# Down projection of a hybrid block: the products M3 and M7 change places in the order of the seven

## The chip, the cores and the metric

The program runs on one core of a Trainium2 chip. The metric is the time of one execution on the device in microseconds. The engines are PE (TensorE; PEld is its weight load), DVE (VectorE), ACT (ScalarE), POOL (GpSimd) and SP (SyncE, which here only issues transfers). Each works through its own list of instructions in order, and semaphores tie the lists together.

## The reference

One block of a hybrid model on 512 tokens of width 2048 in float32: a norm, an input projection, a state-space mixer and a sparse attention side by side, an output projection, and a gated feed-forward network of inner width 5632. The change touches the last product of the last lines alone:

```python
v = rmsnorm(h, ffn_norm_w[l])
h = h + (jax.nn.silu(v @ w_gate[l]) * (v @ w_up[l])) @ w_down[l]
return rmsnorm(h, final_norm_w)
```

## The kernel before

**Seven products.** The feed-forward matrices are multiplied by a scheme of Strassen's kind: a 2 x 2 split of the weights and of the activations, and seven products M1 to M7 instead of eight. The weights of a product are one block of a quad or a sum of blocks: M1 takes 11, M2 takes 12, M6 takes 11 + S1, M3 takes 12 + (11 + S1), M7 takes S3 = 21 + 11, M4 takes 22 and M5 takes S1 = 21 + 22. The sums 11 + S1 and 12 + 11 are made in place on DVE just before the product's form (`q["form"]`, L1422); S1 is made in place on POOL; S3 comes in one of two ways, below.

**Forms.** Float32 precision is kept by splitting each operand in a high part and the rest. The form of a weight block is made by ACT, which writes the high part (`a_hi`, L128), and DVE, which subtracts it for the low part (`lo`, L131). Each 128-row step of a product is then three matmuls: high by high (L1281), high by low (L1282) and low by high (L1283). So a product can start when its high part is there, and needs the low part two matmuls later. `add` (L140) is the helper of all sums on DVE and POOL.

**Visits.** The down projection has 8 column pairs j and 22 stored units n of the gated activations. It is done in 35 visits, each of one j and 3 to 6 units (`VISITS`; they are counted from 0 here). A visit runs its products in the order `SEQ_D`, on four half-filled PSUM banks (`BANK_D`): M1 alone, then M2 and M6, M3 and M7, M4 and M5. A bank is added to H by DVE after the second of its products. Only the last two visits have an order of their own, `SEQ_END`.

**What sets the order.** The instructions of this stage stand in the order in which the code writes them. Before step s runs, `prep(s + 2)` writes the low part of item s + 2 and, ahead of it, the sum and the high part of item s + 3. From visit 3 to visit 22 `ahead` and `room` go one item further where there is space. `late_sum` holds the two items of the first visit that have sums: their sum is written after the low part before them. `advance` (L1169) places the raw blocks in the order of `add_loads`: 11, 12, 21, S3, 22, S1 in the visits of `BY_POOL` (0 to 5 and 22 to 27), and 11, 12, 21, 22, S1, S3 in the others. A block is placed in the space that has been free longest, in Z (38 of 48 column blocks), A2 (6), E (8) or late X (32), and the first block that finds no space holds up all after it. Its load is issued by SP (L1192). In a visit of `BY_POOL`, S3 is an addition on POOL; in another it is a load of 21 by SP and then a transfer issued by POOL that adds 11 to it as it lands (L1194).

**Activations.** `g_forms` makes seven forms of each unit and writes them to `g_d`. A ring of seven slots in SBUF holds the units in use: the first five are loaded by ACT in two parts, pieces 0 to 3 and pieces 4 to 6 (L1675), the others piece by piece by SP (L1693, in `feed`, which runs at the start of each step), in the order of first use. `G_POS` says in which place of a slot the piece of a product lies. Tiles u, V and T are these slots.

Of the kernel before, what the change touches and what calls it, by code (L numbers as in the profile page):

```python
# [17 lines left out]
NP = NFF // 2  # L18
# [30 lines left out]
M1, M2, M3, M4, M5, M6, M7 = range(1, 8)  # L49
# [1 line left out]
SEQ = [M1, M5, M6, M2, M7, M3, M4]  # L51
SEQ_0 = [M1, M2, M5, M6, M7, M3, M4]

SEQ_D = [M1, M2, M6, M3, M7, M4, M5]
BANK_D = {M1: (0, 0), M6: (1, 0), M2: (1, 1), M3: (2, 0), M7: (2, 1), M4: (3, 0), M5: (3, 1)}
V_SLOT = [0, 3, 4, 1, 5, 2, 6]

G_POS = [0, 1, 2, 4, 3, 5, 6]


NA, NZ, NZ2 = 76, 48, 38
# [57 lines left out]
def body(ctx, tc, xT, w_in, w_out, w_gate, w_up, w_down, w1k, w1v, cols, rows, kst, out):  # L119
    nc = tc.nc  # L120
# [3 lines left out]
    def f(ap):  # L124
        return ap.bitcast(F32)

    def a_hi(dst, src, scale=1.0):
        act.activation(dst, src, AF.Copy, scale=scale)  # L128

    def lo(eng, dst, src, hi):  # L130
        eng.tensor_tensor(dst, src, f(hi), ALU.subtract)  # L131

    def neg_lo(dst, src, hi):
        dve.scalar_tensor_tensor(dst, src, -1.0, f(hi), op0=ALU.mult, op1=ALU.subtract)
# [4 lines left out]
    def add(eng, o, a, b):  # L139
        eng.tensor_tensor(o, a, b, ALU.add)  # L140
# [29 lines left out]
    g_d = dram.tile([NP, 7, 128, 512], F32, name="g_d")  # L170
# [1090 lines left out]

    def run_step(s):
        feed(s.i)
        if s.before:
            s.before()
# [267 lines left out]
    def first_gate(u, c, g):  # L1533
        yield 6
        yield from sch.wait(("r", u))
        mul(dve, c, c, g)
        yield from g_forms(u, 3)
# [9 lines left out]
    def g_forms(u, n=0):  # L1547

        ct = P2["CT"].rearrange("p (s c a) t -> p s c (a t)", s=2, c=2)
        g = ct[:, 1]  # L1550
        tg = ct[:, 0].rearrange("p a t -> p (a t)").rearrange("p (a t) -> p a t", a=4)
        sg = P2["ST"][:, 0:14, :].bitcast(F32R).rearrange("p (v s) t -> p v s t", s=2)
        yield 10
        a_hi(sg[:, 0, 0, :], g[:, 0, lo_h])
        a_hi(sg[:, 1:3, 0, :], g[:, 1, :].rearrange("p (a t) -> p a t", a=2), scale=-1.0)
        gq = g.rearrange("p c (a t) -> p (c a) t", a=2)
        if n:
            yield n
        dve.tensor_tensor(tg[:, 1, :], gq[:, 1, :], gq[:, 0, :], ALU.subtract)
        add(dve, tg[:, 2, :], gq[:, 1, :], gq[:, 3, :])  # L1560
        if n:
            yield n
        add(dve, tg[:, 0, :], tg[:, 1, :], gq[:, 3, :])
        dve.tensor_tensor(tg[:, 3, :], tg[:, 0, :], gq[:, 2, :], ALU.subtract)
        yield 4
        lo(dve, sg[:, 0, 1, :], g[:, 0, lo_h], sg[:, 0, 0, :])
        neg_lo(sg[:, 1:3, 1, :], g[:, 1, :].rearrange("p (a t) -> p a t", a=2), sg[:, 1:3, 0, :])
        a_hi(sg[:, 3:7, 0, :], tg)
        yield 4
        if n:  # L1570
            for a in (3, 5):
                lo(dve, sg[:, a:a + 2, 1, :], tg[:, a - 3:a - 1, :], sg[:, a:a + 2, 0, :])
                yield n
        else:
            lo(dve, sg[:, 3:7, 1, :], tg, sg[:, 3:7, 0, :])
        if u < NP - 1:
            for v in range(7):
                yield 8
                nc.sync.dma_start(g_d[u, v], f(sg[:, v]).rearrange("p s t -> p (s t)"))
        else:  # L1580
            yield 16
            nc.scalar.dma_start(g_d[u].rearrange("v p n -> p v n"), f(sg).rearrange("p v s t -> p v (s t)"))
        sch.flags.add(("g", u))
# [78 lines left out]
    G = {}  # L1662
# [3 lines left out]
    def feed(i):  # L1666

        for half, r in ((0, slice(0, 4)), (1, slice(4, 7))):
            while nxt["ring", half] < 5:
                n = nxt["ring", half]  # L1670
                at = done.get((n - GRING, 0), i) + 1 if half == 0 else done.get((4 - GRING, 0), i) + 3 + n // 2
                if at > i:
                    break
                G[n] = P2["slot"][n]
                nc.scalar.dma_start(f(G[n][:, r]).rearrange("p v s t -> p v (s t)"),  # L1675
                                    g_d[n, r].rearrange("v p n -> p v n"))
                nxt["ring", half] += 1
        if not ring:
            for n in range(5, NP):
                for o in range(7):  # L1680
                    ring.append((first_use[n, o], n, o, later[n] if n < GRING else freed[n - GRING, o] + 3))
            ring.sort()
        here = [x for x in ring if x[3] <= i]
        tight = any(x[0] - 8 - i < k for k, x in enumerate(here, 1))
        for x in here[:2 if tight else 1]:
            ring.remove(x)
            u, n, o, _ = x
            assert u > i + 4
            if n == NP - 1 and not o:
                sch.run_until(("g", n))  # L1690
            G[n] = P2["slot"][n % GRING]
            a = G_POS[V_OF[SEQ_D[o]]]
            nc.sync.dma_start(f(G[n][:, a]).rearrange("p s t -> p (s t)"), g_d[n, a])  # L1693
        if not ring:
            ring.append((len(steps) + 99, 0, 0, len(steps) + 99))

# [8 lines left out]
    def g_rhs(p, lo_):  # L1705
        a = G_POS[V_OF[p]]
        return lambda k: (G[lo_ + k][:, a, 0, :], G[lo_ + k][:, a, 1, :])
# [23 lines left out]
    def d_add(j, pr, p, first, last):  # L1731

        H = P2["H"][j]
        p2 = p.rearrange("p (a t) -> p a t", a=2)
        b2 = p[:, None, 0:256].to_broadcast([128, 2, 256])
        if pr == M1:
            if first:
                for i in range(2):
                    act.activation(H[:, i, :], p[:, lo_h], AF.Copy)
            else:  # L1740
                add(dve, H[:, 0:2, :], b2, H[:, 0:2, :])
        elif pr == M6:
            add(dve, H[:, 0:2, :], p2, H[:, 0:2, :])
        elif pr == M7 and first:
            act.activation(H[:, 2:4, :], p2, AF.Copy)
            act.activation(H[:, 4, :], p[:, hi_h], AF.Copy)
        elif pr == M7:
            add(dve, H[:, 2:4, :], p2, H[:, 2:4, :])
            add(dve, H[:, 4, :], p[:, hi_h], H[:, 4, :])
        elif pr == M5:  # L1750
            add(dve, H[:, 3:5, :], p2, H[:, 3:5, :])
            dve.tensor_tensor(H[:, 2, :], H[:, 2, :], p[:, hi_h], ALU.subtract)
# [7 lines left out]
    def d_after(j, first, last):  # L1760
        def after(pr):
            def ev(p):
                d_add(j, pr, p, first, last)
                if last and pr == M6:
                    add_x(j)
                if last and pr == M5:
                    squares(j)
            return ev
        return after
# [49 lines left out]
    def d_end(j, second):  # L1819

        def after(pr):
            def ev(p):
                H = P2["H"][j]
                q = p[:, 0:256]
                if pr == M1:
                    d_add(j, M1, p, False, True)
                    if second:
                        half_mm(0, True)
# [38 lines left out]
    def down_before(v, n):  # L1867
        def before():
            if n == 1:
                assert v < NJ - 2 or not any(fz.busy[NZ2:])  # L1870
                add_h(v)
                if v:
                    P2["A2"] = P2["A"][:, 70:76, :]
            elif n == 0 and v == 27:
                x = GRING * 2 + 1
                assert max(i for i, y in enumerate(visits) if y[1] <= x < y[2]) < v
                close_pool("t0")
                P2["X"] = open_pool("t0", side="right").tile([128, 32, 128], F32, name="X")
            elif (v, n) == (0, 0):
                close_pool("E")  # L1880
                P2["E2"] = P2["E"] = open_pool("E").tile([128, NE, 128], F32, name="E2")
        return before
# [13 lines left out]
    for v, (j, a, b) in enumerate(visits):  # L1896
# [6 lines left out]
        if end >= 0:  # L1903
# [6 lines left out]
            continue  # L1910
        for n, p in enumerate(SEQ_D):
            blk, sums = q["form"][p]
# [4 lines left out]
            if n == 0 and v in (2, 3):  # L1917
                later[5 + (v == 3)] = len(items)
            s = Step(blk, g_rhs(p, a), bk(p), after=af(p),
                     before=down_before(v, n) if n < 2 else None, sums=sums)  # L1920
# [49 lines left out]
    first = pair.evac[0]  # L1970
# [8 lines left out]
    with tc.manual_schedule(engines={mybir.EngineType.PE, mybir.EngineType.Activation, mybir.EngineType.DVE}):  # L1979
        for k in range(KD):  # L1980
            if k % 4 == 0:
                issue_split(k // 2)
            t = xt[:, k, :]
# [115 lines left out]
```

## Time and profile before

| | |
|---|---|
| median of 3 runs | 2162.02 us (2160.78 to 2162.27) |
| the profiled execution | 2162.4 us |
| its span, first to last instruction | 2160.6 us |
| mean granted TensorE clock | 0.997 |
| instructions | 35235 |
| down projection, first matmul | 1688.04 us from the span's start |

In the profile, a group or row names a line of the kernel, the engine, the operation and out<-in by the program's tiles, then shapes. Brackets at the end of a row hold the engine's idle time before it and what ended it. R holds the weights' forms, Z, A, E and X the raw blocks and H, and ps_g, ps_s and ps_t are PSUM banks. Shares of the chain that ended last: PE 88%, DVE 5%, DMA 4%. The transfers read 355.90 MB and wrote 62.39 MB, 194 GB/s over the span.

### The profile page before, as it was taken

The page shows a single profiled execution, that of the slowest core. Times are in us where ns is not written, and L with a number is a line of the kernel's source. Part 1 is how long each engine was busy: PE and PEld are TensorE (multiplying, and loading weights), DVE is VectorE, ACT ScalarE, POOL GpSimd, SP SyncE. Part 2 cuts the span into 40 slices and gives each one's busy share as a digit, 9 for nine tenths or more (in the row PEclk, how much of TensorE's full clock was granted, in tenths as well). Part 3 has the DMA queues.
Part 4 walks back from the last instruction along what each step waited for, and adds up shares of the span by engine and source line. Part 5 has one row for each costly group of instructions (what it writes and reads, how often), then busy time and mean ns, then how long its engine had stood idle before and what let it go on. Part 6 is the DMA issues. An engine that isn't in the chain of part 4 may idle for free.

```text
span 2160.6 us, 35235 instructions
## 1 busy us (share of the span) xinstructions
PE 2130.3 (99%) x12834; PEld 1885.9 (87%) x12834; DVE 1758.4 (81%) x2760; ACT 1221.9 (57%) x2080; POOL 374.1 (17%) x391
## 2 busy tenths in 40 slices
PE   9999999999999999999999999999999899999997
PEld 7888888888888888888888888888888899999997
DVE  6799777868876569888888888888888888888886
ACT  6555456787776656655555556555555454343453
POOL 0002221223211134000000000000000222223232
PEclk9999999999999999999999999999999999999999
DMA  6222343234654487888788887888878879896973
GB/s 215 93 69 74 125 152 97 87 102 134 202 163 118 107 271 218 220 253 239 215 255 231 231 252 214 251 237 220 258 214 267 294 202 316 241 289 165 305 189 107
DMA packets 177470, 426.39 MB, mean 197 GB/s; under 512 B 20720, under 2 KB 25840, under 8 KB 177296
## 3 DMA queue, kind: packets, MB, share of 16 engines
q1 hardware_dynamic: 138816, 320.77, 44.5%
q0 software_dynamic: 29328, 86.00, 20.4%
q10 hardware_dynamic: 9152, 17.36, 2.2%
q8 instruction: 101, 1.65, 0.3%
q14 instruction: 73, 0.60, 0.1%
HBM read 355.90 MB, written 62.39 MB: 194 GB/s over the span
## 4 chain that ended last, share of the span: by engine, by line
PE 88%; DVE 5%; DMA 4%; issue 2%; ACT 1%; POOL 0%; SPq 0%; ACTq 0%; DVEq 0%; POOLq 0%
PE ps_s L1277 21%; PE ps_g L1277 11%; PE ps_g L253 8%; PE ps_g L255 8%; PE ps_g L254 8%; PE ps_t L1277 5%; PE ps_g L1281 2%; PE ps_g L1283 2%; PE ps_g L1282 2%; PE ps_t L1283 2%; PE ps_t L1281 2%; PE ps_t L1282 2%; PE ps_s L1283 2%; PE ps_s L1281 2%; PE ps_s L1282 2%
## 5 line engine op out<-in xcount | busy, mean ns | idle before, releaser
L128 ACT ACTIVATE R<-Z 128x1024 fp32r<-128x1024 f32 (+4 forms) x444 | 407.1, 925 | 392.2 <-DVE Z L140 270.9
L131 DVE TENSOR_TENSOR R<-Z,R 128x1024 fp32r<-128x1024 f32 (+4 forms) x352 | 372.0, 1067 | 46.1 <-ACT R L128 28.3
L253 PE MATMUL ps_g<-u,whi 128*128 128x512 f32 x778 | 317.2, 408 | 0.0
L255 PE MATMUL ps_g<-u,wlo 128*128 128x512 f32 x778 | 306.1, 393 | 0.0
L254 PE MATMUL ps_g<-u,whi 128*128 128x512 f32 x778 | 305.4, 393 | 0.0
L1277 PE MATMUL ps_s<-u,R 128*128 128x512 f32 (+1 forms) x1160 | 251.2, 347 | 0.0
L1277 PEld LDWEIGHTS ps_s<-u,R 128*128 128x128 f32 x1160 | 188.8, 188 | 27.1 <-issue 0.2
L131 DVE TENSOR_TENSOR wlo<-wraw,whi 128x512 fp32r<-128x512 f32 x203 | 142.6, 705 | 59.8 <-ACT whi L128 57.0
L128 ACT ACTIVATE whi<-wraw 128x512 fp32r<-128x512 f32 x203 | 126.0, 624 | 102.6 <-PE ps_g L254 77.5
L255 PEld LDWEIGHTS ps_g<-u,wlo 128*128 128x128 f32 x778 | 146.1, 188 | 31.2
L254 PEld LDWEIGHTS ps_g<-u,whi 128*128 128x128 f32 x778 | 146.8, 189 | 22.6
L253 PEld LDWEIGHTS ps_g<-u,whi 128*128 128x128 f32 x778 | 146.4, 188 | 22.5
L1277 PE MATMUL ps_g<-u,R 128*128 128x512 f32 (+1 forms) x600 | 131.4, 347 | 0.0
L1277 PE MATMUL ps_t<-u,R 128*128 128x512 f32 x592 | 131.2, 348 | 0.0
L1277 PE MATMUL ps_g<-T,R 128*128 128x512 f32 (+1 forms) x584 | 125.9, 346 | 0.2 <-DVE R L131 0.2
L1277 PE MATMUL ps_s<-V,R 128*128 128x512 f32 (+1 forms) x568 | 123.5, 348 | 0.0
L1277 PE MATMUL ps_s<-T,R 128*128 128x512 f32 (+1 forms) x552 | 122.9, 349 | 0.2 <-DVE R L131 0.2
L131 DVE TENSOR_TENSOR E<-Z,R 128x1024 fp32r<-128x1024 f32 (+1 forms) x92 | 111.0, 1207 | 3.4 <-PE ps_t L1277 2.9
L140 DVE TENSOR_TENSOR Z<-Z 128x1024 f32<-128x1024 f32 (+4 forms) x100 | 110.1, 1101 | 4.5 <-POOL Z L140 3.5
L128 ACT ACTIVATE R<-A 128x1024 fp32r<-128x1024 f32 (+3 forms) x72 | 67.9, 943 | 76.5 <-DVE A L140 45.5
L1277 PEld LDWEIGHTS ps_g<-u,R 128*128 128x128 f32 x600 | 98.0, 188 | 14.0
L1277 PEld LDWEIGHTS ps_t<-u,R 128*128 128x128 f32 x592 | 96.9, 188 | 14.0
(520 smaller groups left out, 5489.8 us busy)
## 6 DMA issues: line engine op xcount, KB each, us to landing
Z<-in_w_up SPq DMA_DIRECT2D x95, 512.0 KB, 4.6
Z<-in_w_gate SPq DMA_DIRECT2D x95, 512.0 KB, 5.4
wraw<-in_w_in SPq DMA_DIRECT2D x156, 256.0 KB, 2.6
g_d<-A SPq DMA_DIRECT2D x147, 256.0 KB, 6.4
Z<-in_w_gate POOLq DMA_DIRECT2D x37, 512.0 KB, 7.4
Z<-in_w_up POOLq DMA_DIRECT2D x37, 512.0 KB, 7.8
u<-g_d SPq DMA_DIRECT2D x70, 256.0 KB, 5.2
Z<-in_w_down SPq DMA_DIRECT2D x55, 320.0 KB, 4.6
```

The lines of the kernel that those rows point to most:

```text
L128: act.activation(dst, src, AF.Copy, scale=scale)
L131: eng.tensor_tensor(dst, src, f(hi), ALU.subtract)
L140: eng.tensor_tensor(o, a, b, ALU.add)
L253: pe.matmul(p, hi_t[i][:, j, :], ah, start=(k == 0), stop=False)
L254: pe.matmul(p, hi_t[i][:, j, :], al, start=False, stop=False)
L255: pe.matmul(p, lo_t[i][:, j, :], ah, start=False, stop=(k == u.nk - 1))
L1277: pe.matmul(o, w, x, start=start, stop=(k == n - 1 and o is q), skip_group_check=not fresh[0])
L1281: pe.matmul(q, h[:, k, :], ah, start=(k == 0), stop=False)
L1282: pe.matmul(q, h[:, k, :], al, start=False, stop=False)
L1283: pe.matmul(q, l[:, k, :], ah, start=False, stop=(k == s.blk.n - 1))
```

## The change

M7 is put ahead of M3 in all visits but the last two. The bank that both fill is now added to H after M3. The pieces of M3 and M7 change places in the ring's slots (2 and 5), so that the first part that ACT loads still holds the four pieces that are used first. To that end they are stored in `g_d` in these places, except for the last unit, which is stored in one transfer in the old order and read with the places exchanged.

```diff
-SEQ_D = [M1, M2, M6, M3, M7, M4, M5]
+SEQ_D = [M1, M2, M6, M7, M3, M4, M5]
-G_POS = [0, 1, 2, 4, 3, 5, 6]
+G_POS = [0, 1, 5, 4, 3, 2, 6]
+STORED = [0, 1, 5, 3, 4, 2, 6]
...
-                nc.sync.dma_start(g_d[u, v], f(sg[:, v]).rearrange("p s t -> p (s t)"))
+                nc.sync.dma_start(g_d[u, STORED[v]], f(sg[:, v]).rearrange("p s t -> p (s t)"))
...
-            nc.sync.dma_start(f(G[n][:, a]).rearrange("p s t -> p (s t)"), g_d[n, a])
+            nc.sync.dma_start(f(G[n][:, a]).rearrange("p s t -> p (s t)"),
+                              g_d[n, STORED[a] if n == NP - 1 else a])
...
-        elif pr == M7 and first:
+        elif pr == M3 and first:
...
-        elif pr == M7:
+        elif pr == M3:
             add(dve, H[:, 2:4, :], p2, H[:, 2:4, :])
             add(dve, H[:, 4, :], p[:, hi_h], H[:, 4, :])
```

The new code is one line longer above line 1694 and two below it, so L131, L140, L1192, L1194 and L1693 of before are L132, L141, L1193, L1195 and L1694 there.

DVE at the first visit, before, from the sum for M6 (Z<-Z) on; the rows R<-Z,R are the low parts of M6, M3, M7 and M4, the second Z<-Z is the sum for M3, and the rows on A in between belong to the end of the gate and up projections:

```order
L140 TENSOR_TENSOR Z<-Z 128x640
L137 TENSOR_TENSOR A<-A,rrow 128x1024
L140 TENSOR_TENSOR A<-ps_g,A 128x256
L137 TENSOR_TENSOR A<-A 128x1024
L131 TENSOR_TENSOR R<-Z,R 128x640
L140 TENSOR_TENSOR Z<-Z 128x640
L131 TENSOR_TENSOR R<-Z,R 128x640
L1559 TENSOR_TENSOR A<-A 128x256
L140 TENSOR_TENSOR A<-A 128x256 x2
L1564 TENSOR_TENSOR A<-A 128x256
L131 TENSOR_TENSOR R<-Z,R 128x640
```

The same place on DVE now:

```order
L141 TENSOR_TENSOR Z<-Z 128x640
L138 TENSOR_TENSOR A<-A,rrow 128x1024
L141 TENSOR_TENSOR A<-ps_g,A 128x256
L138 TENSOR_TENSOR A<-A 128x1024
L132 TENSOR_TENSOR R<-Z,R 128x640 x2
L141 TENSOR_TENSOR Z<-Z 128x640
L1560 TENSOR_TENSOR A<-A 128x256
L141 TENSOR_TENSOR A<-A 128x256 x2
L1565 TENSOR_TENSOR A<-A 128x256
L132 TENSOR_TENSOR R<-Z,R 128x640
```

The low parts of M6 and M7 stand together, the sum for M3 follows them, and M3's low part comes three rows later.

SP before visit 10, before, from the load of its block 22 (the row of E) through that of its S3 (the first row of Z) to the first load of visit 11 (the second row of Z); the rows of T are pieces of the ring:

```order
L1192 DMA E_15819<-in_w_down 128x640
L1693 DMA T_8425<-g_d 128x512
L1693 DMA T_8429<-g_d 128x512
L1192 DMA Z<-in_w_down 128x640
L1693 DMA T_8425<-g_d 128x512
L1693 DMA T_8429<-g_d 128x512
L1693 DMA T_8425<-g_d 128x512
L1693 DMA T_8429<-g_d 128x512
L1693 DMA T_8425<-g_d 128x512
L1192 DMA Z<-in_w_down 128x640
```

The same place on SP now, from block 22 (the first row of Z) through S3 (the second) to the first two loads of visit 11 (E and A):

```order
L1193 DMA Z<-in_w_down 128x640
L1694 DMA T_8425<-g_d 128x512
L1694 DMA T_8429<-g_d 128x512
L1694 DMA T_8425<-g_d 128x512
L1694 DMA T_8429<-g_d 128x512
L1694 DMA T_8425<-g_d 128x512
L1193 DMA Z<-in_w_down 128x640
L1694 DMA T_8429<-g_d 128x512
L1193 DMA E_15819<-in_w_down 128x640
L1193 DMA A<-in_w_down 128x640
```

S3's load has gone behind block 22, which takes the space that S3 had, and behind five loads of the ring, up to where visit 9's S3 is read for the last time.

POOL in visits 12 to 17, before; the additions are the visits' S1, the transfers of L1194 write S3, and those of A from h_d belong to H:

```order
L140 TENSOR_TENSOR Z<-Z 128x640
L1194 DMA Z<-in_w_down 128x640
L140 TENSOR_TENSOR Z<-Z 128x640
L1194 DMA E_15819<-in_w_down 128x640
L1703 DMA A<-h_d 128x1024
L140 TENSOR_TENSOR Z<-Z,A 128x640
L1194 DMA Z<-in_w_down 128x640
L1703 DMA A<-h_d 128x1024
L140 TENSOR_TENSOR Z<-Z 128x640
L1194 DMA Z<-in_w_down 128x640
L140 TENSOR_TENSOR A<-A,Z 128x640
L1194 DMA E_15819<-in_w_down 128x640
```

The same visits on POOL now:

```order
L141 TENSOR_TENSOR Z<-Z 128x640
L1195 DMA E_15819<-in_w_down 128x640
L141 TENSOR_TENSOR Z<-Z 128x640
L1195 DMA E_15819<-in_w_down 128x640
L1705 DMA A<-h_d 128x1024
L141 TENSOR_TENSOR Z<-Z 128x640
L1195 DMA E_15819<-in_w_down 128x640
L1705 DMA A<-h_d 128x1024
L141 TENSOR_TENSOR Z<-Z 128x640
L1195 DMA E_15819<-in_w_down 128x640
L141 TENSOR_TENSOR Z<-Z 128x640
L1195 DMA E_15819<-in_w_down 128x640
```

The instructions are the same and stand in the same order, but S3 lies in E in every one of these visits.

## The prediction

> **What bounds the kernel now.** I read the page first, then the trace in stretches of 13 us, then who PE waits for.
>
> ```profile
> span 2160.6 us, 35235 instructions
> PE 2130.3 (99%) x12834; PEld 1885.9 (87%) x12834; DVE 1758.4 (81%) x2760; ACT 1221.9 (57%) x2080; POOL 374.1 (17%) x391
> ```
>
> PE is idle for only 30.3 us of the span. The visits that change run from 1688 us to about 2118 us, so only PE's idle time there can be won, and everything else can only be lost. The stretches (columns: window, length, busy PE, PEld, DVE, ACT, POOL with their counts, PE clock, DMA share, GB/s):
>
> ```profile
> 1692.00:1705.00 13.00, 8.50 (x56) 8.20 (x57) 10.53 (x16) 7.56 (x15) 3.10 (x3) 0.87 0.79 265
> 1809.00:1822.00 13.00, 13.00 (x113) 13.00 (x112) 12.11 (x19) 5.61 (x8) 1.99 (x1) 1.00 0.93 303
> 1848.00:1861.00 13.00, 13.00 (x112) 13.00 (x111) 12.11 (x18) 5.02 (x7) 3.63 (x4) 1.00 0.87 197
> 1887.00:1900.00 13.00, 13.00 (x112) 13.00 (x111) 10.96 (x16) 5.54 (x8) 2.45 (x2) 1.00 1.03 318
> 2030.00:2043.00 13.00, 12.05 (x99) 11.65 (x99) 12.07 (x19) 4.85 (x7) 4.52 (x4) 1.00 1.05 375
> ```
>
> PE is full between 1720 and 2000, but DVE works 11 to 12 of 13 us and the DMA engines stand at 0.87 to 1.03: PE bounds, and both others are close behind. PE's waits in 1680 to 1700, in 1700 to 1720, and from 2000 to the end:
>
> ```profile
> PE ps_t L1283 <- DVE R L131: 3.2, 1, 3.2
> PE ps_t L1281 <- ACT R L128: 1.6, 1, 1.6
> ...
> PE ps_s L1283 <- DVE R L131: 1.2, 1, 1.2
> PE ps_g L1283 <- DVE R L131: 1.1, 1, 1.1
> ...
> PE ps_t L1283 <- DVE R L131: 1.5, 4, 0.7
> PE ps_s L1283 <- DVE R L131: 0.9, 3, 0.5
> PE ps_g L1283 <- DVE R L131: 0.5, 1, 0.5
> ```
>
> L1283 is a product's third matmul, the first that needs the low part that DVE makes in L131. The 1.6 and 3.2 us stand at M6 of the first visit, ahead of the first place that changes: they stay. The rest, 1.2 + 1.1 and 1.5 + 0.9 + 0.5, is 5.2 us: more than that cannot be gained.
>
> **What is gained.** No instruction is added or removed. M3's form (a sum on DVE, the high part on ACT, the low part on DVE) is made one product later and M7's (S3, no sum) one earlier. The bank that both share is still added up after the second of them. The stored pieces keep their number, their 256 KB and their places on SP, which I cost at nothing: their cover is the ring, which loads each piece more than four products ahead of its use; a late one would cost at most its own landing.
>
> Rows of DVE and POOL at the first two visits and at visit 26:
>
> ```profile
> 1698.54 0.83 DVE L131 TENSOR_TENSOR R<-Z,R 128x640 fp32r<-128x640 f32 x1 [0.86 <-ACT R L128]
> 1704.69 1.69 POOL L140 TENSOR_TENSOR Z<-Z 128x640 f32<-128x640 f32 x1 [8.43 <-DMA Z<-in_w_down]
> 1704.89 2.64 DVE L131 TENSOR_TENSOR R<-Z,R 128x640 fp32r<-128x640 f32 x2
> 1709.91 0.55 DVE L140 TENSOR_TENSOR Z<-Z 128x384 f32<-128x384 f32 x1
> 1710.38 2.38 DVE L131 TENSOR_TENSOR R<-Z,R 128x384 fp32r<-128x384 f32 x2
> ...
> 2020.28 0.68 DVE L140 TENSOR_TENSOR Z<-Z 128x512 f32<-128x512 f32 x1
> 2020.88 0.68 DVE L131 TENSOR_TENSOR R<-Z,R 128x512 fp32r<-128x512 f32 x1
> ```
>
> In the first visit DVE idles 0.86 us because M3's high part waits for M3's sum; M7's low part, which now stands there, waits for no sum. The low parts at 1704.89 then start 0.86 us earlier, ahead of POOL's addition that stretches them (2.64 for two, against 0.83 for one), and the wait of 1.2 goes. In the second visit the sum of 0.55 no longer stands ahead of M6's low part, and I take 0.7 of the 1.1. Together 1.9 us, between 0.9 (the idle time alone) and 2.3. In the late visits it is the same: the sum at 2020.28 stands right ahead of the low part that PE waits for. Of the 2.9 us there, the longest wait, 0.7, stands at an M2, ahead of the change, and stays, and so may some short ones: 2.0 us, between 1.0 and 2.9. **Gain 3.9 us, between 1.9 and 5.2.** What is late next is S3.
>
> **What is lost.** In visits 6 to 21 and 28 to 34, S3 is brought by two transfers in a row: SP's load of 21 (L1192), and POOL's accumulating transfer of 11 onto it (L1194). Visit 11, from the load to PE:
>
> ```profile
> 1817.12 0.33 SPq L1192 DMA_DIRECT2D A<-in_w_down  x1
> 1818.61 1.99 POOL L140 TENSOR_TENSOR Z<-Z 128x640 f32<-128x640 f32 x1 [12.05 <-DVE R L131]
> 1822.38 0.88 POOL L1194 DMA_DIRECT2D A<-in_w_down  x1 [1.78 <-DMA A<-in_w_down]
> 1830.89 0.74 ACT L128 ACTIVATE R<-A 128x640 fp32r<-128x640 f32 x1 [3.17 <-DMA A<-in_w_down]
> 1831.67 0.83 DVE L131 TENSOR_TENSOR R<-A,R 128x640 fp32r<-128x640 f32 x1 [2.49 <-ACT R L128]
> 1830.16 0.28 PE L1281 MATMUL ps_t<-u,R 128*128 128x256 f32 x1
> 1831.94 0.28 PE L1281 MATMUL ps_t<-u,R 128*128 128x256 f32 x1
> 1832.55 0.38 PE L1283 MATMUL ps_t<-u,R 128*128 128x256 f32 x1 [0.20 <-DVE R L131]
> ```
>
> From the load's issue to the low part's end it takes 15.4 us, and PE already waits 0.2. The two L1281 rows are the starts of M3 and M7: one product is 1.78 us, a visit of seven 12.46. M7 in M3's place is wanted 1.78 us earlier.
>
> The load is not issued earlier. It goes out when its space is free, at the same point of the program as before; on POOL the accumulation keeps its place, and POOL's order shows where S3 lies: in visits 12 to 19 every S3 now lies in E, which has 8 column blocks where an S3 takes 5. So a load waits until DVE has made the previous visit's M7, which itself waited for its transfers: a loop through SP, POOL, ACT and DVE, once per visit. Before, the space came from the form one place ahead of M7, which waits for no transfer, 8 products before its use. Time to landing of L1192 and L1194 in 1796 to 1842, then in 1842 to 1930:
>
> ```profile
> DMA to landing us min/median/max: 2.9/4.8/5.9
> DMA to landing us min/median/max: 5.7/6.9/8.4
> ...
> DMA to landing us min/median/max: 3.0/4.5/7.7
> DMA to landing us min/median/max: 5.8/8.0/8.3
> ```
>
> Loop at the medians: 4.5 + 0.5 to POOL's issue (1822.38 against 1817.12 + 4.7) + 8.0 + 1.7 for high and low part (1830.89 to 1832.50, and 0.1 between) = 14.7 us; at the short ends 3.0 + 0.5 + 5.8 + 1.7 = 11.0. A visit has 12.46. And where M7's low part is late, M3's sum, the addition of a bank and M3's low part (0.83 + 0.68 + 0.83) follow it on DVE against 1.78 us of PE: about 0.6 us more.
>
> The Trainium skill (DMA: Bandwidth & Descriptors, Anatomy of one DMA) fits a GpSimd-issued transfer at 2.0 us plus its bytes over 436 thousand per us, an estimate of 2.75 us for 320 KB. The trace does not agree: 5.7 to 8.4 here. By the fit the loop would take 9.5 us (4.5 + 0.5 + 2.75 + 1.7), nothing would be late, and the sum would be 2158.1.
>
> Visit 10 is the first hit; its S3 load moves behind five loads of T:
>
> ```profile
> 1799.49 0.33 SPq L1192 DMA_DIRECT2D Z<-in_w_down  x1
> 1802.58 0.69 DVE L131 TENSOR_TENSOR R<-Z,R 128x512 fp32r<-128x512 f32 x1 [0.78 <-ACT R L128]
> 1803.19 2.06 DVE L140 TENSOR_TENSOR Z<-Z 128x512 f32<-128x512 f32 x1
> 1817.96 0.28 PE L1283 MATMUL ps_s<-u,R 128*128 128x256 f32 x1
> ```
>
> It went out at 1799.49; now it waits for visit 9's M7, whose low part follows the one at 1802.58, two evacuations and POOL's addition (which stretches the sum at 1803.19 to 2.06): 1805.4. Then 4.8 + 0.5 + 6.9 + 1.7 gives 1819.3, with 8.4 for the accumulation 1820.8; PE wants it at 1817.96. I take 2.0 us. In visit 11 the load of 22 hangs on that same late low part, and POOL's addition with it (1.99) stands ahead of the accumulation: 4.8 + 2.0 + 6.9 + 1.7 = 15.4, less 12.46: 2.9. Visit 12 the same in a thinner stretch: 2.2, and 0.6 behind it. Visits 13 and 14 have the short ends (DMA 0.87): 0. Visits 15 to 19 would lose 14.7 - 12.46 = 2.2 each at today's density; but a slower PE thins the traffic, so I take 0.8 each, less 1.3 of lead, and 0.6 behind: 3.3. **Loss 11.0 us.** At the short ends everywhere it is 0 (visit 10 at 1816.2); at the long ends 3 + 4.3 + 4.3 + 11 + 1.2 = 24.
>
> **The sum.** The profiled execution took 2162.4 us (span 2160.6 and 1.8 around it): 2162.4 - 3.9 + 11.0 = 2169.5. The median of the runs is 0.4 lower: **2169.1**.
>
> **Rivals.** *S3 comes in time, and the change is no loss.* If load and accumulation together stay under 10.3 us (12.46 less 0.5 and 1.7), as at the short ends, the loop never binds and the gain is left: 2158.1 on the median, 2156.8 with all 5.2 us. For it: the 0.2 at 1832.55 is PE's only wait for an S3 in the rows above, and a slower PE thins the traffic. Against it: the medians, and E as the only space. With a loop that binds in two or three visits it ends between 2158 and 2166.
>
> *PE's pauses halve its clock.* After the waits of 1.6 and 3.2 us the granted clock is 0.87 in the 13 us of 1692 to 1705, 1.7 us lost. If the waits of visits 10 to 12 do that too, the time is 2169.1 + 3 x 1.7 = 2174.2. Against it: mine are 2 to 3 us. The Trainium skill (TensorE: Matmul & The Clock Gate, The HAM clock gate) puts the drop behind an idle window of about 3.4 us; by that rule these pauses cost no clock, while the trace shows one after 3.2.
>
> *The change does not do what it says*: excluded, the order shows M7's form ahead of the sum in the first visit.
>
> **How the numbers follow.** Forecast 0.50, clock 0.13, S3 in time 0.37 (0.27 without a measurable change, 0.10 with nearly all the gain). About 0.2%, 4.3 us, is what a measurement here can tell from none: faster 0.10, same 0.27, slower 0.63. The range goes down to 2159.5, into the third case as far as 1.4 us of loss, and up to 2178.5, past the clock's case to a loss of 20 of the 24 us.
>
> **What would show it.** Right: in 1805 to 1930 ACT waits for `DMA E<-in_w_down` in most visits, and PE for L131's successor by 1 to 3 us at M7 in visits 10 to 12; the waits of 1.2 and 1.1 are gone, and those after 2000 fall to about 1 us. Wrong: PE full between 1800 and 1930 (then the accumulation lands within 6 us, or the load leaves earlier than I say), or waits at the start that only moved.

## The result, and the profile after

The changed kernel took 2174.72 us (median of 4 runs, 2173.52 to 2178.42), beside 2161.5 us for the kernel before on the same chip: a ratio of 1.0062, 95% interval 1.005 to 1.0074. It is slower by 13.2 us, where 7.1 were forecast. The profiled execution took 2173.52 us and is compared with the 2162.4 us of the one before.

The page of the changed kernel, its span and the busy times:

```profile
span 2171.5 us, 35229 instructions
PE 2136.2 (98%) x12834; PEld 1892.4 (87%) x12834; DVE 1761.9 (81%) x2760; ACT 1218.9 (56%) x2080; POOL 373.8 (17%) x391
```

PE has the same 12834 matmuls, but is busy for 5.9 us more and idle for 5.0 us more (35.3 against 30.3). The clock was lower, too: 0.994 against 0.997 on the mean. Both show in the stretches of 13 us (columns as before):

```profile
1809.00:1822.00 13.00, 10.82 (x76) 10.41 (x76) 7.64 (x12) 4.21 (x6) 1.87 (x2) 0.87 0.73 234
1848.00:1861.00 13.00, 11.42 (x94) 11.06 (x93) 10.78 (x16) 4.85 (x7) 3.10 (x4) 1.00 0.77 189
1887.00:1900.00 13.00, 12.67 (x107) 12.46 (x106) 10.68 (x15) 4.53 (x7) 1.75 (x2) 1.00 0.83 252
2030.00:2043.00 13.00, 12.68 (x106) 12.38 (x105) 10.79 (x16) 4.74 (x7) 3.53 (x3) 1.00 1.04 378
```

In the first of them PE was busy for all 13 us before, with 113 matmuls; now there are 76, a clock of 0.87, and a DMA share of 0.73 in place of 0.93. Whom PE waits for in 1800 to 1945, where it waited 0.2 us before:

```profile
PE ps_s L1282 <- ACT R L129: 2.5, 2, 1.8
PE ps_g L1284 <- DVE R L132: 2.3, 4, 1.2
PE ps_t L1282 <- ACT R L129: 1.4, 1, 1.4
PE ps_s L1284 <- DVE R L132: 1.1, 3, 0.4
PE ps_t L1284 <- DVE R L132: 0.6, 2, 0.4
```

Together they are 7.9 us. (All lines of this kernel from 59 to 1693 stand one further down than before, later ones two.) In 1700 to 1720 the view of waits has no row left: the 1.2 and the 1.1 us are gone. The timeline at visit 10's S3, from the load to PE:

```profile
1802.26 0.33 SPq L1193 DMA_DIRECT2D Z<-in_w_down  x1
1809.07 0.88 POOL L1195 DMA_DIRECT2D Z<-in_w_down  x1 [2.74 <-DVE A L141]
1816.08 0.74 ACT L129 ACTIVATE R<-Z 128x640 fp32r<-128x640 f32 x1 [5.20 <-DMA Z<-in_w_down]
1816.85 0.83 DVE L132 TENSOR_TENSOR R<-Z,R 128x640 fp32r<-128x640 f32 x1 [4.18 <-ACT R L129]
1816.87 0.38 PE L1282 MATMUL ps_s<-u,R 128*128 128x256 f32 x1 [1.82 <-ACT R L129]
1817.73 0.58 PE L1284 MATMUL ps_s<-u,R 128*128 128x256 f32 x1 [0.36 <-DVE R L132]
```

Read from the bottom: PE waits for ACT, ACT has been idle 5.2 us for a transfer, and the transfer was issued by POOL only when the load before it had landed, at 1808.51. (The bracket at 1809.07 names an addition on DVE that ended within 0.1 us of this landing.) The transfers are what is late, and no engine's work. In 1842 to 1945 the accumulating transfers of seven visits, all into E, each waited for their load:

```profile
L1195 POOL DMA_DIRECT2D E<-in_w_down x7: 877/877/880, 1852.9 to 1931.9; - x7
...
  DMA E<-in_w_down: 24.9, 7
...
DMA to landing us min/median/max: 4.6/6.8/7.6
```

And ACT, which in 1805 to 1930 waited once, for 0.8 us, for a transfer into E before, now does so six times:

```profile
ACT R L129 <- DMA E<-in_w_down: 13.6, 6, 3.6
```

A load that waits for its space stands at the head of SP's list, and every load behind it waits too. SP's transfers at visit 10, two rows that follow each other:

```profile
1810.05 0.32 SPq L1694 DMA_DIRECT2D u<-g_d  x1
1817.70 0.33 SPq L1193 DMA_DIRECT2D Z<-in_w_down  x1
```

The load at 1817.70 leaves when DVE has made M7's low part (1816.85 + 0.83). One visit later it is the same: SP stands from 1825.57 until that visit's accumulating transfer lands at 1832.19, and the load leaves at 1833.92, behind M7's low part. SP's line of loads in 1802 to 1842, and the traffic in 40 equal parts of that stretch:

```profile
L1193 SPq EVENT_SEMAPHORE  x14: 17/17/6652, 1804.5 to 1841.0; - x14
```

```profile
GB/s 386 373 388 392 389 396 362 394 391 381 302 228 246 56 18 0 54 248 395 334 381 171 334 347 175 264 285 246 292 271 29 0 20 207 405 360 353 384 290 372
```

The longest of these waits is 6.65 us, the one from 1825.57 (4.13 before). Around 1815 to 1818 and 1832 to 1834 the traffic falls to nothing, and then all goes out in one burst, with the next S3 in it.

What a visit costs is best read from the first matmul of each visit. In the timeline of before, M1 of visit 10 and of visit 20:

```profile
1812.42 0.28 PE L1281 MATMUL ps_t<-u,R 128*128 128x256 f32 x1
...
1937.28 0.28 PE L1281 MATMUL ps_g<-u,R 128*128 128x256 f32 x1
```

and of after:

```profile
1809.54 0.28 PE L1282 MATMUL ps_t<-u,R 128*128 128x256 f32 x1
...
1948.43 0.28 PE L1282 MATMUL ps_g<-u,R 128*128 128x256 f32 x1
```

The changed kernel comes to visit 10 2.88 us earlier and to visit 20 11.15 us later: 14.0 us are lost in ten visits. By visits, from the same rows:

| visit | lost | of it waits of PE | predicted |
|---|---|---|---|
| 10 | 4.2 | 2.2 | 2.0 |
| 11 | 3.4 | 1.8 | 2.9 |
| 12 | 2.2 | 1.6 | 2.2 + 0.6 |
| 13, 14 | 1.3 | 0.6 | 0 |
| 15 to 19 | 3.0 | 1.7 | 3.3 |

The waits are 7.9 of the 14.0 us, and 3.4 are two stretches of 3.41 us at half the clock, in visits 10 and 11 (below). The rest stands for the most part at the waits too, since the view counts a wait from the modelled end of the matmul before: from 1816.87 to 1817.73 above it is 0.86 us from the first to the third matmul of M7, 0.62 more than without a wait (0.24, at 1809.54), and the view shows 0.36.

And the late visits, 2012 to 2080, where 2.9 us of waits were to fall to about 1:

```profile
PE ps_t L1282 <- ACT R L129: 1.9, 1, 1.9
PE ps_t L1284 <- DVE R L132: 0.9, 3, 0.4
PE ps_s L1282 <- ACT R L129: 0.7, 1, 0.7
PE ps_s L1284 <- DVE R L132: 0.4, 1, 0.4
```

They rose to 3.9. Three questions were left: is it the space of S3 that makes it late, what does the clock cost, and what stands in the late visits.

### The profile page after: what moved, and what is told of

It is laid out like the page before. It is cut to its first block, busy times and chain, and to the rows that moved or that the text cites. A ratio compares the mean times of both kernels' runs of the same rounds, so it can differ in the third digit from the quotient of the medians.

```text
span 2171.5 us, 35229 instructions
## 1 busy us (share of the span) xinstructions
PE 2136.2 (98%) x12834; PEld 1892.4 (87%) x12834; DVE 1761.9 (81%) x2760; ACT 1218.9 (56%) x2080; POOL 373.8 (17%) x391
## 5 line engine op out<-in xcount | busy, mean ns | idle before, releaser
L132 DVE TENSOR_TENSOR R<-Z,R 128x1024 fp32r<-128x1024 f32 (+4 forms) x349 | 376.8, 1090 | 54.4 <-ACT R L129 36.6
L132 DVE TENSOR_TENSOR wlo<-wraw,whi 128x512 fp32r<-128x512 f32 x203 | 143.1, 708 | 60.2 <-ACT whi L129 57.0
L132 DVE TENSOR_TENSOR E<-Z,R 128x1024 fp32r<-128x1024 f32 (+1 forms) x92 | 111.1, 1208 | 3.6 <-PE ps_t L1278 3.1
L141 DVE TENSOR_TENSOR Z<-Z 128x1024 f32<-128x1024 f32 (+4 forms) x99 | 108.8, 1099 | 3.8 <-POOL Z L141 3.2
L1278 PEld LDWEIGHTS ps_t<-u,R 128*128 128x128 f32 x592 | 97.0, 188 | 13.9
```

The source lines that it names most:

```text
L1278: pe.matmul(o, w, x, start=start, stop=(k == n - 1 and o is q), skip_group_check=not fresh[0])
```

## Where gain and loss lie, and S3's space

All edits are to the changed kernel. The medians of before in the four sets of runs were 2161.63, 2161.70, 2162.13 and 2162.49 us. Two kernels take the new order in some visits only:

```diff
+SEQ_NEW, SEQ_OLD = [M1, M2, M6, M7, M3, M4, M5], [M1, M2, M6, M3, M7, M4, M5]
+NEW = list(range(6)) + list(range(22, 28))      # the other kernel: range(6, 22)
-        for n, p in enumerate(SEQ_D):
+        for n, p in enumerate(SEQ_NEW if v in NEW else SEQ_OLD):
```

(The ring's table goes by product in place of place, and the shared bank is added after whichever of M3 and M7 is second.) In visits 0 to 5 and 22 to 27:

> The new order only in the visits whose S3 is made by POOL's addition (0 to 5 and 22 to 27), the old order in visits 6 to 21 and 28 to 32; the stored places as in the changed kernel. Theory (gain and loss lie in different visits): the first visits' 2.6 us and the 2.1 us of visits 25 to 27 are gained and nothing is lost: 2161.5 - 4.7 = 2156.8, between 2155.5 and 2158.5. Rival (a PE that is 2.6 us ahead runs into its loads in visits 10 to 19): the 2.6 are given back there as waits at M7, 2159 to 2160. Rival (the ring's places or the stored places carry part of the loss): above 2162.

2159.81 us (10 runs), ratio 0.9994, interval 0.9984 to 1.0003: 1.3 us above the theory's range and in that of the first rival, but not by its cause. PE has no wait at all in 1800 to 1945, and from visit 0 to visit 10 it takes 121.40 us against 124.38: the gain holds, the old order in the middle loses nothing, and the ring and the stored places cost nothing. (The profiled execution, 2164.29 us, was the longest of the ten, so only differences inside the stage are read from it.) But from visit 28 to visit 30 it gives back 3.75 us, with the old order there: see the late visits below.

In visits 6 to 21 alone:

> The new order only in visits 6 to 21, the old order in all others. Theory (loop): the loss alone, 13.7 us by the changed kernel's trace from visit 9 to visit 20, less up to 2.6 because PE comes 2.6 us later to visit 10: 2172.5 to 2175.2, with the periods between the low parts of M7 in visits 10, 11 and 12 at 15 to 16 us again. Rival (the loss needs the gain in front of it, PE being early): under 2166.

2175.26 us (4 runs), ratio 1.0066, interval 1.0051 to 1.0081. The total is at the upper end of what was foreseen, the split is not: 7.8 us are lost from visit 6 to 20 (177.50 us against 169.72), 1.7 of them in visit 7, where the changed kernel loses none, and 3.7 from visit 25 on, where the order is the old one; why there stays open. In visit 10 PE does not wait: it comes there 4.6 us later than in the changed kernel, and S3 only 1.1 us later. Visit 11 has 2.5 us of waits again and a period (from one low part of M7 to the next) of 16.3 us:

```profile
PE ps_t L1283 <- ACT R L130: 2.2, 1, 2.2
```

So the rival was partly right: in visit 10 what had been gained at the start was itself turned into a wait. From visit 12 to 20 only 2.2 us are lost too, against 6.4 in the changed kernel, but there S3 lies in other spaces, so this run does not say why. S3 of visits 12 to 19 lies in Z here, and yet each of its loads leaves within 0.1 us of the end of the M7 low part of the visit before (in visit 12 at 1835.11, where the low part ends at 1835.09). So it is the hand-over from one S3 to the next that makes the loop, and not E as such; with a load of 3.1 us and an accumulating transfer of 6.0 us in visit 12 it is just short enough not to bind.

Then the order of the loads, so that S3 takes a space freed some four products earlier:

```diff
-        add_loads(q, "11 12 21 S3 22 S1" if v in BY_POOL else "11 12 21 22 S1 S3")
+        add_loads(q, "11 12 21 S3 22 S1")
```

> The changed kernel, but in every visit the loads of S3 stand ahead of 22 in the list of loads (as the visits by POOL have it already), so that S3 takes a space that came free some 4 products earlier and no longer the one that the previous visit's M7 frees. Theory (the loop through S3's space): PE's waits at M7 and M3 in visits 10 to 19, 7.9 us, and the low clock behind two of them fall away, some 12 of the 13.7 us lost there: 2161 to 2164 us, and with 22 loaded later M6 may wait for S1 by up to 0.5 us a visit. Rival (the transfers are too long in this traffic, wherever they lie): within 3 us of the changed kernel's 2174.7. Rival (22 is now the late one: M6 waits 1 to 2 us in most visits): 2168 to 2178 with the waits at M6.

2165.81 us (7 runs), ratio 1.0026, interval 1.0015 to 1.0037: 8.9 us less than the changed kernel, a little over the upper end of the theory. The waits of PE in 1800 to 1945 are these:

```profile
PE ps_t L1282 <- ACT R L129: 0.9, 1, 0.9
PE ps_t L1284 <- DVE R L132: 0.7, 2, 0.4
PE ps_g L1282 <- ACT R L129: 0.5, 1, 0.5
PE ps_g L1284 <- DVE R L132: 0.4, 1, 0.4
PE ps_s L1284 <- DVE R L132: 0.3, 1, 0.3
```

and all of them lie before 1838: from there to 1945 the view is empty. Visits 12 to 19 take 99.56 us, as before (99.57; 106.0 in the changed kernel). The new order costs nothing there where S3's space comes early. What is left is visits 10 and 11 (4.0 us; S3 of visit 11 still takes the space of visit 10's M7: its load leaves at 1818.15, and that M7's low part ends at 1818.13), visit 7 (1.4 us, with a wait of 0.5 at M6, whose S1 needs the later 22: the second rival, in one visit), and the late visits.

## What the clock costs

The profile shows where the clock fell. In the windows view of after, in steps of 3.41 us:

```profile
1814.15:1817.56 3.41, 1.40 (x10) 0.99 (x8) 0.71 (x1) 0.74 (x1) 0.00 (x0) 1.00 0.26 83
1817.57:1820.98 3.41, 3.25 (x15) 3.25 (x16) 3.13 (x6) 2.23 (x4) 0.00 (x0) 0.50 0.65 203
...
2066.74:2070.15 3.41, 2.39 (x21) 2.18 (x19) 1.65 (x3) 2.21 (x4) 0.86 (x1) 1.00 0.03 8
2070.15:2073.56 3.41, 2.21 (x16) 2.01 (x17) 2.55 (x5) 3.41 (x6) 0.74 (x1) 1.00 0.48 82
```

One granted clock of 0.50 for 3.41 us is 1.7 us lost. The pause of 1.82 + 0.36 us in visit 10 is followed by such a stretch, and so is the one of 1.45 + 0.35 in visit 11; the pause of 1.86 + 0.35 at 2069 is not. The same kernel was run once more:

> The changed kernel once more, for a second profile of it. Theory (loop): the periods from low part to low part of M7 in visits 10 to 12 are again over 14 us each, PE waits again 1 to 2.5 us at M7 in at least two of them, and where PE's busy share of one of the clock's windows of 3.41 us falls under a half the clock is 0.50 in the next; 2172 to 2178 us. Rival (the transfers of that one profile were slow by chance): periods under 13.5 and 2165 to 2170.

2174.64 us (4 runs), ratio 1.0066, interval 1.0051 to 1.0081, periods of visits 10 to 12 of 15.5, 15.8 and 15.2 us: as foreseen. Here the pause of visit 10 (1.99 + 0.36) falls across two windows and costs no clock, and the one at 2069.6 lies in one:

```profile
1813.40:1816.81 3.41, 2.01 (x17) 1.81 (x16) 0.23 (x1) 0.20 (x1) 0.00 (x0) 1.00 0.71 183
1816.81:1820.22 3.41, 2.46 (x17) 2.19 (x17) 2.55 (x4) 1.70 (x3) 0.00 (x0) 1.00 0.27 75
...
2069.40:2072.81 3.41, 1.03 (x6) 0.63 (x5) 1.21 (x2) 3.41 (x7) 0.87 (x1) 1.00 0.44 77
2072.81:2076.22 3.41, 3.41 (x18) 3.41 (x17) 3.38 (x6) 2.19 (x4) 1.24 (x1) 0.50 0.55 138
```

Two things follow. With the clock at 0.50 in visit 10 or without, M1 of visit 12 starts at 1842.42 and 1842.43 (visit 10 at 1809.54 and 1809.91): in this pair a slow PE inside the loop cost next to nothing, since the next S3 was waited for anyway. Outside it the 1.7 us are lost: visit 29 takes 16.9 us in the second profile and 15.2 in the first.

To take the pauses away, PE got small matmuls to do in them, into the bank that M7 then overwrites:

```diff
         p, q, *fresh = s.psum()
+        for _ in range({397: 7, 404: 7}.get(s.i, 0)):
+            pe.matmul(q[:, 0:128], ones, ones, start=True, stop=True)
```

Items 397 and 404 are M7 of visits 10 and 11.

> The changed kernel with seven small matmuls (128x128, ones by ones, 0.22 us each at full clock by the first ones of the program) put into M7's own bank ahead of M7 in visits 10 and 11, so that PE works through 1.5 us of the two pauses; M7 overwrites them. Theory (loop): the granted clock behind the two pauses stays at 1.00, but M7 of the next visit ends when its own chain of transfers does, so that what the clock gives back stands as a longer wait at the next M7: the time within 1.7 us of 2174.7 (only the last of the two, 1.7 us, may be won). Rival (the clock's loss adds up): 2 x 1.7 us won or more, 2171.3 or less. Rival (the clock falls all the same): clock 0.6 behind the pauses, 2174.7.

2169.97 us (4 runs), ratio 1.0041, interval 1.0026 to 1.0056. The clock stayed at 1.00, but 4.7 us were won where I had allowed 1.7: my theory fell on the sum. The profile says where: the period of visit 11 was 13.9 us (16.2 in the changed kernel; that of visit 12, 14.7, was not shorter than its 14.5), and no wait was left between visit 12 and visit 23. Three more kernels were to tell whether that was chance: the same again, the seven in visit 10 alone (`{397: 7}`), and one in visit 10 (`{397: 1}`), which moves the program but leaves the pause.

> The changed kernel with the seven small matmuls ahead of M7 in visits 10 and 11 once more, for a second profile. The first took 4.7 us less than the changed kernel, where the loop let 1.7 at most be expected: the periods from low part to low part of M7 in visits 11 and 12 were 13.9 and 14.7 us (15.4 to 16.4 in three profiles without the filling), and the waits behind visit 12 were gone. Theory A (a full clock of PE really shortens the loop): periods under 15 again and the waits of visits 13 to 19 gone again, 2167 to 2172 us. Theory B (that run's transfers were fast by chance): periods of 15.2 or more, 2173 or more.

> The same with the seven small matmuls in visit 10 alone. Theory A (each window of the clock that is saved counts, and the loop behind it gets shorter): 2171 to 2173 us, a shorter period of visit 11 than 15. Theory B (the loop gives back what the clock gains: the wait at M7 in visit 11 grows from 1.8 to about 3.4 us and takes the clock with it there): 2174 to 2176, a period of 15.4 to 16.4.

> One small matmul ahead of M7 in visit 10 in place of seven: the program is moved as with the filling, the pause stays. In three profiles with the filling the first loads behind visit 10's M7 landed 2.9 to 3.1 us after their issue and visit 11's period was 13.9 to 14.7 us, in three without it 3.1 to 4.5 and 15.8 to 16.4. Theory A (the pause of PE makes the difference): a period of 15.4 or more, 2173 to 2177 us. Theory B (only the program's other place in memory and in time does it): a period under 15, 2169 to 2173.

| | median, us | visit 11: period, us | its load of S3, us |
|---|---|---|---|
| changed kernel, two profiles | 2174.72, 2174.64 | 16.2, 15.8 | 4.8, 4.8 |
| one matmul in visit 10 | 2176.33 (2 runs) | 15.8 | 4.6 |
| seven in visit 10 | 2172.66 | 14.1 | 3.8 |
| seven in visits 10 and 11 | 2169.97, 2171.35 | 13.9, 14.7 | 3.5, 4.0 |

The period is read from the starts of M7's low parts, here with seven matmuls in visit 10:

```profile
1818.12 0.83 DVE L132 TENSOR_TENSOR R<-Z,R 128x640 fp32r<-128x640 f32 x1 [4.02 <-ACT R L129]
...
1832.19 0.83 DVE L132 TENSOR_TENSOR R<-Z,R 128x640 fp32r<-128x640 f32 x1 [1.61 <-ACT R L129]
```

and with one:

```profile
1820.21 0.83 DVE L132 TENSOR_TENSOR R<-Z,R 128x640 fp32r<-128x640 f32 x1 [3.98 <-ACT R L129]
...
1835.99 0.83 DVE L132 TENSOR_TENSOR R<-Z,R 128x640 fp32r<-128x640 f32 x1 [3.01 <-ACT R L129]
```

By the first matmuls, visits 10 and 11 take 29.2 to 29.8 us in the three profiles with seven matmuls, 31.5 with one, and 32.9 and 32.5 in the changed kernel. In visit 12 the repeat fell short of theory A: its period was 15.2 us, with the clock at 0.50 behind it. And visits 12 to 19 took 101.9, 104.0 and 103.7 us with the filling, but also 103.8 with the one matmul (106.0 and 105.1 in the changed kernel), so that part of the gain is not the filling's alone.

So three profiles of three have the shorter visit 11, which speaks against chance, and the program's place doesn't make it (theory B of the last kernel falls, by one profile). But theory A isn't shown either: the clock is not the cause, since the second profile of the changed kernel had a full clock behind visit 10 and a period of 15.8; and the missing pause alone is not, since the kernel with the new order in 6 to 21 had no pause in visit 10 and yet a load of 4.9 us and a period of 16.3. What seven small matmuls ahead of M7 do to the transfers behind it stays open.

## The late visits

At visit 29, M7's high part is not late because of S3, which landed at 2059.94. The timeline of after, POOL and ACT:

```profile
2056.77 1.81 POOL L141 TENSOR_TENSOR Z<-Z 128x768 f32<-128x768 f32 x1 [2.32 <-DMA Z<-in_w_down]
...
2059.12 1.18 POOL L1726 DMA_DIRECT2D acc<-rrow  x1
...
2067.94 0.63 ACT L1724 ACTIVATE rrow<-A 128x512 f32<-128x512 f32 x1 [2.17 <-DMA acc<-rrow]
2068.48 0.62 ACT L1724 ACTIVATE A<-A 128x512 f32<-128x512 f32 x1
2069.00 1.32 ACT L129 ACTIVATE A<-A,colc 128x512 f32<-128x512 f32 x2
2070.22 1.35 ACT L129 ACTIVATE R<-X 128x640 fp32r<-128x640 f32 x2
```

From visit 27 to 32 every visit finishes a block of rows, and `squares` then puts 2.3 us of ACT's work right ahead of the next M7's high part (2070.22). At 2067.94 it waits for a transfer that adds the squares before, which POOL issued behind an addition that itself waited 2.32 us for a load. The test puts the squares one product later:

```diff
                 if last and pr == M5:
-                    squares(j)
+                    P2["later"] = j
...
+                if pr == M1 and "later" in P2:
+                    squares(P2.pop("later"))
```

> The changed kernel with the squares of a finished block of rows one product later on ACT (behind the next visit's M1, no longer behind its own M5), so that they stand behind the high part of the next visit's M7 and no longer ahead of it. Theory (at M7 of visits 28 and 29 PE waits for squares, which wait for M5's addition and for the accumulating transfer of the squares before): the 1.1 and 2.2 us there fall away and at most 0.5 comes back at M3, 2 to 3 us less than the changed kernel in the same shots, 2171.5 to 2173 by the earlier median. Rival (M3's form, now right behind the squares, is as late as M7's was): within 1 us of the changed kernel, the waits at M3. The visits before 27 as in the changed kernel.

2173.16 us (4 runs), ratio 1.0056, interval 1.0041 to 1.0071; 1.5 us under the changed kernel of the same set, where 2 to 3 were foreseen, and the runs overlap. The profile, which lost 2.0 us more in visits 10 to 19 than that of the changed kernel, tells more: visits 27 to 29 take 37.98 us against 40.24, and the waits of 2012 to 2080 are now

```profile
PE ps_s L1284 <- DVE R L132: 1.3, 1, 1.3
PE ps_t L1284 <- DVE R L132: 1.0, 2, 0.5
```

The wait at visit 29 is gone, the one at visit 28 has become a wait for the low part. So squares, not S3, held M7 there.

## A version that beats both

> The kernel with the new order in visits 0 to 5 and 22 to 27 only, and the squares one product later. Theory: of the 4.3 us that the visits 28 and 29 gave back there, 3 or more are saved, 2159.8 - 3 = 2157, between 2155.5 and 2158.5, faster than before by 0.15 to 0.3%. Rival (the waits only move to the next product): 2159 to 2161.

This is the kernel with the new order in visits 0 to 5 and 22 to 27, with the later squares: 2160.03 us (10 runs), ratio 0.9995, interval 0.9986 to 1.0005, above the theory's range. With the old order in 28 to 32 the later squares only moved the waits, as the rival had it: 3.6 us are given back between visits 28 and 34.

> The new order in all visits but 6 to 21 (0 to 5 and 22 to 32), and the squares one product later. Theory (the loss lies in visits 6 to 21 alone): all of the gain that was foreseen at the two ends, 2.6 + 2.0: 2156 to 2158, like the kernel with the old order in 28 to 32 or 0.5 us less, since a sum no longer stands ahead of M7's low part. Rival (S3 is late in visits 28 to 32 too once the squares are out of its way): 2159 or more with waits at M7 there.

2157.93 us (10 runs), ratio 0.9983, interval 0.9973 to 0.9992. With the new order in 28 to 32 too nothing is given back: from visit 28 to visit 34 it takes as long as before (78.02 us), and from visit 0 to visit 28 it had taken 2.3 us less. In 1700 to 2012 a single wait of 0.5 us is left. This one is faster than both kernels, by 3.8 and 16.7 us on the medians.

> The new order in all visits but 6 to 11, S3's loads ahead of 22 in visits 12 to 21, the squares one product later. Theory (the loss in visits 12 to 21 comes from S3's late space alone, the order itself costs nothing there): no wait of PE between visits 10 and 22, and the time of the kernel with the old order in 6 to 21, 2158, between 2156 and 2160. Rival (the order costs more in the dense visits than S3's space): waits of PE at M7 or M6 in visits 12 to 21, 2161 to 2168.

Here the new order stands in visits 12 to 21 as well, with S3's loads ahead of 22: 2159.74 us (10 runs), ratio 0.9987, interval 0.9977 to 0.9996. In 1705 to 2012 PE waits 0.4 us, once, in visit 11, and the profiled execution, 2156.1 us, was the shortest of all these runs. Visits 12 to 19 take 99.59 us. The order itself costs nothing there, and gains nothing; it was the space of S3 that cost.

## Why the prediction came out as it did

It was right on the sign and on the mechanism, and its range held the time; its change of +7.1 us was 6.1 too small. 2.1 of these lie between profile and medians: the profiled execution of before was 0.9 us over its median of these runs, the one of after 1.2 under. The other 4.0 are 3.0 more of loss, 2.0 less of gain in the late visits, and 1.0 more of gain at the start:

- **Gain at the start**, 1.9: both waits went, and PE is 2.9 us ahead at visit 10, though that execution came 0.7 us later to the stage. Right, a little small, and in part luck: 0.6 us of it is a shorter wait at M6 of the first visit, which the prediction let stand and which the kernel with the old order there shows as well. In the second profile of the changed kernel 0.8 us of the two waits is left.
- **Gain in the late visits**, 2.0: none. Up to visit 28 2.0 us were gained, in visits 28 to 30 2.1 were lost. The step that failed is "the sum stands right ahead of the low part that PE waits for": true of those waits, but what was late next there was not looked for. It was ACT's squares, in front of the high part that was now wanted one product earlier.
- **S3's loop**, 11.0: 14.0. The line of transfers, the space E and the visits were named rightly. For visit 10 2.0 us of lateness were taken and 2.6 came, by errors that cancel: the load left at 1802.26, not 1805.4, took 6.2 us to land, not 4.8, and PE wanted S3 2.9 us earlier than the row used, because of the gain in front; the term took gain and loss as independent. To the 2.6 us the half clock added 1.6. Visit 11 was close by other terms than those named: POOL's addition ended at 1822.56, before S3's load had landed (1823.43), so its 2.0 us did not stand in the chain; the period of 16.2 is 0.9 until the load left, 4.8, 0.6 to POOL's issue, 8.2 for the accumulation and 1.7. The term of the visits 13 and 14, 0 at "the short ends", was mis-sized: the accumulating transfers took 6.9 us there, not 5.8, and 1.3 us were lost. Visits 15 to 19 were right (3.0 for 3.3).
- **"Mine are 2 to 3 us"**, the reason against the clock rival: wrong. Pauses of 1.8 and 2.2 us halved the clock, in visits 10 and 11, but not in 12. Its price, 1.7 us each on top of the forecast, did not hold either: in the two profiles of the changed kernel visit 12 starts at the same time with the half clock in visit 10 and without. Its 2174.2 is close to the time measured for a reason that the two profiles of the changed kernel contradict.
- **S3 in time**: not in visits 10 to 12; from visit 13 on it was nearly so, and what PE waited for there was mostly M3's low part behind a late M7, as the term of 0.6 had it.

## What to carry to other kernels

Before an operand is wanted earlier, look at what frees the space that it is loaded into: if that is the same operand of the round before, the load, the transfers and the forms make a loop, and its period has to stay under the round's. A gain ahead of such a place isn't free: PE comes earlier to a transfer that does not. And where a wait is to go, look in the engine's queue for what stands just ahead of the work that will be waited for next.

## What the runs showed of the hardware

**The clock's windows.** In every profile all stretches at 0.50 begin on one grid of 3.413 us: in after at 537.57, 1694.69, 1817.57 and 1834.63, which are 339, 36 and 5 steps apart. In the fourteen profiles of this study, up to the last 20 us, each of the 24 windows at full clock in which PE was busy for 0.45 of the time or less was followed by one at 0.50, and none in which it was busy for 0.57 or more; between them it went both ways. So a pause of about 2 us costs 1.7 us of clock or nothing, by where it falls; at visit 29 this moved the time by 1.7 us between two executions of one kernel. The Trainium skill (TensorE: Matmul & The Clock Gate, Part 1: The HAM clock gate) speaks of free-running windows of about 3.4 us, and the traces agree; it asks for an idle window, and here one in which PE was idle for 0.55 of the time was enough every time.

**Small matmuls and transfers.** The load of S3 behind visit 10's M7 took 4.6 to 5.0 us in the five profiles with the new order and S3 last in the loads, and 3.5 to 4.0 in the three of these kernels in which seven small matmuls had filled PE's pause ahead of that M7, though in the one of each that were laid side by side the transfers issued ahead of it were the same, at the same distances. No run here says why.
